# Output projections of the last two token blocks ahead of the rest of an FFN, and an RMS scaling that reads PSUM

## The chip, the cores and the metric
The kernel runs on one core of a Trainium2 chip. Times are device microseconds of one execution, from the first instruction to the last. The kernel before was timed in three runs: median 3093.57 us, 3091.24 to 3095.78.

## The reference, cut to what matters
One decoder layer on 2048 tokens of width 1024, in float32, with a final norm:

```python
h = rms_norm(x, norm1_g)
p = h @ w_in                                   # combined projection of three head groups
mix = concat(mlstm(p), rwkv7(p), diff_attn(p)) # 256 + 256 + 512 columns
x = x + mix @ w_out
h = rms_norm(x, norm2_g)
x = x + square(relu(h @ w_ff_up)) @ w_ff_down  # 1024 -> 4096 -> 1024
return rms_norm(x, final_g)
# rms_norm(x, g) = x * rsqrt(mean(x*x, -1) + eps) * g
```

## The kernel before
Activations stand transposed: features on the 128 partitions, tokens along the free axis. The 2048 tokens are four blocks c = 0..3 of T = 512, and the trunk's state of a block is eight tiles `x` of 128 x 512. A float32 product is made of three products of rounded float32 (`mm3`, lines 182 to 184, and `prod`, lines 1223 to 1225): each operand is split into a high part (ACT, line 174) and a low part (POOL or DVE, line 175), and hi·hi, lo·hi and hi·lo are summed in one PSUM bank. So weights take a path of their own: a load of 128 x 512 (`wraw`, class `Weights`, three raw buffers, six of `whi` and `wlo`), ACT, POOL, TensorE.

The first two thirds make the projection and the three head groups. Attention of blocks 2 and 3 runs at the same time as the FFN of blocks 0 and 1 (class `Tail`): `outproj` (line 1113) makes x + mix @ w_out of one block, 192 products with a residual tile (`traw`, loaded at line 1121) added at line 1126; `hidden` the norm; `ffn` the up products (tile `pd`, line 1162) and down products (tile `py`, added into x at line 1174) of sixteen feature groups fb; `final` (line 1185) the last norm and the stores. `norm` takes squares on ACT (lines 155, 158), adds them on DVE (159), sums over partitions on TensorE with a matrix of ones (162), makes the reciprocal root (164, 134 to 137), spreads it over the partitions by a product with a diagonal matrix (144, 145), copies that out of PSUM (168) and scales (1194 on DVE, 1191 and 1192 on ACT and POOL).

Blocks 2 and 3 come last, and their FFN is made with a Strassen-Winograd scheme of seven products per step (class `Wino`) on the 2 x 2 blocks made of token block and feature half. `first(x2)` norms block 2; `second` norms block 3 (scalings at line 1231) and makes the token operands: differences such as t2 = b11 + (b22 - b12) (lines 1256 to 1272), each split into high and low. `up` runs eight steps with weights in a ring `wr` of 512 KB tiles (loads `wr<-in_wu`; differences of weights at lines 1286 to 1293), `down` four steps with `wr` and a second ring `wr2` (`wr<-in_wd`), token tiles read back from DRAM (`x<-act`), and sums `acc`. The tail of `down` is `final(2)` and `final(3)`.

The order in which each engine runs its instructions is fixed when the program is built: a scheduler takes instructions by priority, and those under `tc.high_priority()` come as soon as their operands and buffers allow by its own reckoning. Each engine then runs its list strictly in order. A buffer is reused when its last reader is through. Memory is given out in pools: a pool opened after another is closed takes its place, and its first writes wait for the readers of what stood there. Before, attention's memory is free at fb = 8 of `ffn(x1)`, by when the pools `wr`, `tx2` and `th2` take it; the two out-projections are generators that are stepped between the feature groups 9 to 15 and share the weight ring and the `traw` ring with the FFN. Loads are issued from the queues of SP and ACT (line 42).

## Time and profile before

| what | us |
|---|---|
| median of three runs | 3093.57 |
| lowest, highest | 3091.24, 3095.78 |
| the profiled execution | 3098.3 |
| its span (first to last record) | 3096.6 |

The engines' busy shares of that span are PE 94%, DVE 63%, ACT 42%, POOL 35%. The profile is of one execution, so its stretches add up to its own time. Times in the rows count from the span's start. FFN(x1) ends at about 2363.4 us, up runs from there to 2714, down to 3062.5. A matrix product of the rows below that lasts 0.39 us is issued every 0.23 us, since they overlap; to count them, divide a full stretch by its number of products. [...]

### The profile page before, as it was taken

To read this page: it belongs to the slowest core of one execution; us is meant where nothing else is said; L and a number is where in the kernel's file an instruction comes from. 1 tells how busy PE (TensorE), PEld (TensorE's weight loads), DVE (VectorE), ACT (ScalarE), POOL (GpSimd) and SP (SyncE) were. 2 spreads that over 40 slices of the span, in tenths; PEclk is the share of its full clock that TensorE was granted. 3 is DMA by queue.
4 is the path that set the end of the run, shared out by engine and by line. 5 is a ranking of instruction groups with operands and counts; after the bars stand their busy time and mean duration, and the time that the engine had idled before them with its cause. 6 is when DMAs were issued, how large, how long until landed. Compare 5 with 4: busy or idle time off the path is not lost. (4 is left out here: it accounts for less than half of the span.)

```text
span 3096.6 us, 47520 instructions
## 1 busy us (share of the span) xinstructions
PE 2898.9 (94%) x16848; PEld 2376.1 (77%) x16848; DVE 1947.5 (63%) x4355; ACT 1297.8 (42%) x2571; POOL 1069.5 (35%) x1023
## 2 busy tenths in 40 slices
PE   8999999999999889999999999987996899979996
PEld 7886887778878667888888788876784688858884
DVE  6587878678772556555555756443435756657787
ACT  5343234323322445444444544443343545434433
POOL 4344444333333114333433333323453322112232
PEclk9999999999999899999999999998998999989998
DMA  8445332643543553533446334424442344474431
GB/s 298 134 136 199 86 98 74 215 120 89 184 127 117 163 140 99 138 101 103 123 113 169 96 106 119 109 69 140 130 140 78 106 150 159 140 258 146 143 116 55
DMA packets 317096, 409.15 MB, mean 132 GB/s; under 512 B 102421, under 2 KB 164150, under 8 KB 315834
## 3 DMA queue, kind: packets, MB, share of 16 engines
q1 hardware_dynamic: 229002, 283.81, 30.0%
q10 hardware_dynamic: 87856, 122.31, 13.0%
q8 instruction: 133, 2.18, 0.3%
q14 instruction: 105, 0.86, 0.1%
HBM read 298.24 MB, written 107.76 MB: 131 GB/s over the span
## 5 line engine op out<-in xcount | busy, mean ns | idle before, releaser
L175 POOL TENSOR_TENSOR wlo<-wraw,whi 128x512 fp32r<-128x512 f32 (+2 forms) x432 | 591.6, 1381 | 825.4 <-ACT whi L174 545.4
L174 ACT ACTIVATE whi<-wraw 128x512 fp32r<-128x512 f32 (+2 forms) x432 | 267.1, 625 | 336.9 <-PE pd L183 98.5
L175 POOL TENSOR_TENSOR wlo<-wr,whi 128x512 fp32r<-128x512 f32 x104 | 148.6, 1430 | 486.6 <-ACT whi L174 401.4
L182 PE MATMUL pd<-hh,whi 128*128 128x512 f32 x768 | 303.2, 399 | 12.2 <-ACT hh L174 12.1
L183 PE MATMUL pd<-hl,whi 128*128 128x512 f32 x768 | 303.9, 396 | 0.0
L1174 DVE TENSOR_TENSOR x<-py,x 128x512 f32<-128x512 f32 x256 | 174.5, 688 | 203.8 <-PE py L184 203.2
L184 PE MATMUL pd<-hh,wlo 128*128 128x512 f32 x768 | 299.9, 395 | 0.0
L1030 DVE TENSOR_SCALAR_CACHE_REDUCE E<-pS 128x512 f32<-128x512 f32 (+4 forms) x320 | 185.8, 607 | 153.3 <-PE pS L1027 87.5
L174 ACT ACTIVATE whi<-wr 128x512 fp32r<-128x512 f32 x224 | 140.1, 630 | 273.6 <-PE pd L1224 135.8
L182 PE MATMUL pd<-hhi,whi 128*128 128x512 f32 x544 | 224.2, 416 | 7.4 <-ACT hhi L279 7.4
L184 PE MATMUL pd<-hhi,wlo 128*128 128x512 f32 x544 | 223.5, 413 | 0.2 <-POOL wlo L175 0.2
L183 PE MATMUL pd<-hlo,whi 128*128 128x512 f32 x544 | 223.2, 412 | 0.4 <-POOL hlo L175 0.3
L182 PE MATMUL py<-ah,whi 128*128 128x512 f32 x512 | 205.7, 402 | 1.5 <-DVE x L1174 1.1
L183 PE MATMUL py<-al,whi 128*128 128x512 f32 x512 | 202.6, 396 | 0.6 <-DVE al L175 0.6
L184 PE MATMUL py<-ah,wlo 128*128 128x512 f32 x512 | 200.8, 396 | 0.0
L1037 ACT ACTIVATE E<-E,nm 128x128 f32<-128x128 f32 (+15 forms) x128 | 153.7, 1201 | 96.0 <-DVE nm L1033 80.1
L182 PE MATMUL pd<-whi,hhi 128*128 128x256 f32 (+1 forms) x640 | 188.3, 295 | 1.3 <-ACT gates L372 1.3
L183 PE MATMUL pd<-wlo,hhi 128*128 128x256 f32 (+1 forms) x640 | 188.4, 294 | 0.0
L184 PE MATMUL pd<-whi,hlo 128*128 128x256 f32 (+1 forms) x640 | 187.0, 292 | 0.0
L1056 PEld LDWEIGHTS pO<-Vt,PT 128*128 128x128 f32 x1088 | 151.9, 202 | 36.1 <-ACT PT L1053 25.8
L182 PEld LDWEIGHTS pd<-hh,whi 128*128 128x128 f32 x768 | 144.9, 190 | 43.9 <-issue 12.5
L1056 PE MATMUL pO<-Vt,PT 128*128 128x128 f32 x1088 | 160.4, 290 | 18.8 <-ACT PT L1053 18.8
(445 smaller groups left out, 7204.5 us busy)
## 6 DMA issues: line engine op xcount, KB each, us to landing
act<-x SPq DMA_DIRECT2D x96, 256.0 KB, 2.1
wraw<-in_wu ACTq DMA_DIRECT2D x64, 256.0 KB, 3.2
wraw<-in_wu SPq DMA_DIRECT2D x64, 256.0 KB, 3.1
wraw<-in_wd ACTq DMA_DIRECT2D x64, 256.0 KB, 3.3
wraw<-in_wd SPq DMA_DIRECT2D x64, 256.0 KB, 3.1
x<-act SPq DMA_DIRECT2D x56, 256.0 KB, 2.8
x<-act ACTq DMA_DIRECT2D x56, 256.0 KB, 2.8
wraw<-in_wi ACTq DMA_DIRECT2D x48, 256.0 KB, 3.5
```

What stands on the lines that cost most here:

```text
L174: nc.scalar.activation(hi, src, AF.Copy)
L175: lo_eng.tensor_tensor(lo, src, hi.bitcast(F32), ALU.subtract)
L182: nc.tensor.matmul(out, sh, mh, start=(i == 0), stop=False)
L183: nc.tensor.matmul(out, sh, ml, start=False, stop=False)
L184: nc.tensor.matmul(out, sl, mh, start=False, stop=(i == n - 1))
L1030: V.tensor_scalar(E[:, k0:k0 + w], s_[:, :w], 0.125, None, ALU.mult, ALU.max, accum_out=mb[:, j:j + 1])
L1037: A.activation(E[:, :n], E[:, :n], AF.Exp, bias=nm, accum_out=l)
L1056: PE.matmul(o[:, 0:P], pt[:, b * P:(b + 1) * P], vt[:, kb], start=(kb == 0), stop=(kb == i))
L1174: nc.vector.tensor_tensor(x2[d], ps, x2[d], ALU.add)
```

## The change
The out-projections of blocks 2 and 3 are no longer stepped through `ffn(x1)`. At fb = 8 both are written one after the other, with a `Weights` object of their own (pool `tw2` in attention's memory, two raw buffers) and a ring `xr` of three for residual and mixed tiles. The norms of x2 and x3 and the operands b11, b21, t2 and t3 (`first`, `second`) follow right behind them, ahead of the rest of `ffn(x1)`. The operands t4, t1 and c22 are made by a new `third` behind `final(1)`. The ring `wr` takes the place of `tw2` and has five buffers rather than six. In `down` the token splits use the pool `th2` rather than one of their own, four groups of token tiles are in use rather than five, and the sixth group of sums stands in a freed slot. The last two norms are written out: `squares` takes the squares of finished sums during the last step, `rstd` sums them on TensorE (also over several tiles in one accumulation) and `scale` multiplies straight from the PSUM tile of the broadcast, block 2 on DVE alone, block 3 with two of its eight tiles on POOL. All stores there are issued by SP.

```diff
--- before.py
+++ after.py
@@ -187,8 +187,8 @@
-    def __init__(s, tc, e, wp, bufs=6, width=512):
-        s.tc, s.e, s.wp, s.bufs, s.width = tc, e, wp, bufs, width
+    def __init__(s, tc, e, wp, bufs=6, width=512, raws=3):
+        s.tc, s.e, s.wp, s.bufs, s.width, s.raws = tc, e, wp, bufs, width, raws
@@ -198,7 +198,7 @@
-                raw = s.wp.tile([P, s.width], F32, name="wraw", tag="wraw", bufs=3)
+                raw = s.wp.tile([P, s.width], F32, name="wraw", tag="wraw", bufs=s.raws)
@@ -1082,7 +1082,7 @@
-        s.hp = p(s.hctx, "th", bufs=10)
+        s.hp = p(s.hctx, "th", bufs=8)
@@ -1098,26 +1098,27 @@
-    def load(s, c, pool=None):
+    def load(s, c, pool=None, raw=None):
...
         for k in range(KT):
-            r = s.raw()
+            r = (raw or s.raw)()
...
-    def outproj(s, c, m, x2, g, pd=None, keep=None):
+    def outproj(s, c, m, x2, g, w=None, raw=None, pd=None, keep=None):
...
+        get = (w or s.w).get
         for u in range(4):
-            w = s.w.get(s.wo[u], 256)
+            w = get(s.wo[u], 256)
             for j in range(2):
                 d = 2 * u + j
-                xr = s.raw()
+                xr = (raw or s.raw)()
...
-    def second(s, x2, x3, hp, tp):
+    def second(s, x2, x3, hp):
 
...
         with s.tc.high_priority():
             s.rms(x3)
-            b11, b21, b12, b22 = x2[:4], x2[4:], x3[:4], x3[4:]
-            t2, t3, t1, t4 = [], [], [], []
+            b11, b12, b22 = x2[:4], x3[:4], x3[4:]
+            s.t2, s.t3 = t2, t3 = [], []
             for k in range(4):
                 V.tensor_tensor(b12[k], b22[k], b12[k], ALU.subtract)
                 V.tensor_tensor(b11[k], b12[k], b11[k], ALU.add)
                 t2 += s.cut(b11[k:k + 1], [tl.hl(hp)], (V,))
             for k in range(4):
-                t3 += s.cut(b12[k:k + 1], [tl.hl(hp)], (G, V))
+                t3 += s.cut(b12[k:k + 1], [tl.hl(hp)], (V,))
+
+    def third(s, x2, x3, tp):
...
+        with s.tc.high_priority():
+            b11, b21, b12, b22 = x2[:4], x2[4:], x3[:4], x3[4:]
+            t1, t4 = [], []
             for k in range(4):
                 V.tensor_tensor(b21[k], b21[k], b11[k], ALU.subtract)
                 t4 += s.cut(b21[k:k + 1], [tl.hl(tp)], (V,))
             for k in range(4):
                 V.tensor_tensor(b12[k], b22[k], b11[k], ALU.subtract)
                 t1 += s.cut(b12[k:k + 1], [(tl.slot(2, F32R), tl.slot(3, F32R))], (V,))
-            c22 = s.cut(b22, [tl.hl(), tl.hl()] + [(tl.slot(1, F32R), tl.slot(1, F32R)) for _ in range(2)], (G, V))
-        s.ops = [s.b11, t2, s.b21, t3, t1, t4, c22]
+            c22 = s.cut(b22, [tl.hl(tp), tl.hl(tp)] + [(tl.slot(1, F32R), tl.slot(1, F32R)) for _ in range(2)], (G, V))
+        s.ops = [s.b11, s.t2, s.b21, s.t3, t1, t4, c22]
...
 
@@ -1309,7 +1318,7 @@
             with tc.high_priority():
-                w = s.blocks(s.wr, 6, [tl.wu[fb + 8 * m][:, 4 * k:4 * k + 4] for m in range(2) for k in range(2)])
+                w = s.blocks(s.wr, 5, [tl.wu[fb + 8 * m][:, 4 * k:4 * k + 4] for m in range(2) for k in range(2)])
...
-    def down(s, ap, ar, wr2):
+    def down(s, ap, hp, wr2):
...
-        grp = [2, 3, 0, 4, 5]
...
-        acc = [[ap.tile([P, T], F32, name="acc", tag=f"a{p}{q}") if p < 6 else tl.slot(1) for q in range(4)] for p in range(7)]
+        grp = [2, 3, 0, 4]
...
+        acc = [[ap.tile([P, T], F32, name="acc", tag=f"a{p}{q}") if p < 5 else tl.slot(5 if p == 5 else 1) for q in range(4)] for p in range(7)]
         with tc.high_priority():
             for p, c, d in ((2, 0, 0), (5, 0, 4), (6, 1, 0)):
                 for q in range(4):
@@ -1383,8 +1392,8 @@
             with tc.high_priority():
-                f = [s.factors(s.blocks(r, b, [tl.wd[2 * st + i + 8 * k][:, :, T * m:T * m + T] for m in range(2) for k in range(2)]))
-                     for i, (r, b) in enumerate(((s.wr, 6), (wr2, 5)))]
+                f = [s.factors(s.blocks(r, 5, [tl.wd[2 * st + i + 8 * k][:, :, T * m:T * m + T] for m in range(2) for k in range(2)]))
+                     for i, r in enumerate((s.wr, wr2))]
@@ -1396,7 +1405,7 @@
                 for k in range(4):
...
                         w = s.unit(ws[k // 2][:, k % 2 * T:k % 2 * T + T], V if k % 2 else G)
-                        b = (ar.tile([P, T], F32R, name="uh", tag="uh"), ar.tile([P, T], F32R, name="ul", tag="ul"))
+                        b = tl.hl(hp)
@@ -1414,9 +1423,61 @@
-                if last and p == 5:
-                    tl.final(2, acc[2] + acc[5], (1, 5))
-        tl.final(3, acc[6] + x22, (2, 4, 7))
+                    if last and p == 2:
+                        n2 = s.squares(tl.np.tile([P, T], F32, name="nacc", tag="nacc", bufs=1), acc[2], True)
+                    if last and p == 4:
+                        n3 = s.squares(ap.tile([P, T], F32, name="nacc"), x22, True)
+                    if last and p == 5:
+                        s.squares(n2, acc[5], False)
+                        r2 = s.rstd([n2], 1)
+        with tc.high_priority():
+            sq = [n3]
+            for q in range(4):
+                sq.append(tl.slot(2))
+                A.activation(sq[-1], acc[6][q], AF.Square)
+            s.scale(3, x22 + acc[6], s.rstd(sq, 0), tl.slot(3), (1, 3))
+        s.scale(2, acc[2] + acc[5], r2, None, ())
+
+    def squares(s, n, x, new):
...
+        nc = s.tc.nc
+        for i, t in enumerate(x):
+            y = n if new and i == 0 else s.tl.raw()
+            nc.scalar.activation(y, t, AF.Square)
+            if y is not n:
+                nc.vector.tensor_tensor(n, n, y, ALU.add)
+        return n
+
+    def rstd(s, sq, i):
...
+        nc, e, tl = s.tc.nc, s.e, s.tl
+        ps = s.bank(i)
+        for j, t in enumerate(sq):
+            for tt in range(4):
+                nc.tensor.matmul(ps[:, tt:tt + 1], t[:, tt * P:(tt + 1) * P], e.ones[:, 0:1], start=j + tt == 0, stop=j == len(sq) - 1,
+                                 skip_group_check=True)
+        sm = tl.np.tile([P, 3, 4], F32, name="nsm", tag="nsm", bufs=2)
+        nc.vector.tensor_scalar(sm[:, 0], ps[:, 0:4], 1.0 / D, NORM_EPS, ALU.mult, ALU.add)
+        rsqrt(nc, e, sm[:, 1], sm[:, 0], sm[:, 2])
+        ps = s.bank(i)
+        bcast_rows(nc, e, tl.raw(), ps, sm[:, 1])
+        return ps
+
+    def scale(s, c, x, r, t, pool):
...
+        nc, e, tl = s.tc.nc, s.e, s.tl
+        g = lambda k: e.vf[:, V_FG + k:V_FG + k + 1]
+        order = [(k + 4) % KT if c == 3 else k for k in range(KT)]
+        for i in pool:
+            nc.scalar.activation(x[i], x[i], AF.Copy, scale=g(order[i]))
+        if pool:
+            nc.scalar.copy(t, r)
+        for i, k in enumerate(order):
+            if i in pool:
+                nc.gpsimd.tensor_tensor(x[i], x[i], t, ALU.mult)
+            else:
+                nc.vector.scalar_tensor_tensor(x[i], x[i], g(k), r, ALU.mult, ALU.mult)
+            nc.sync.dma_start(tl.out[c, :, k], x[i])
 
@@ -1540,33 +1601,29 @@
             actx.close()
             with tc.using_default_side("right"):
                 pq = [ctx.enter_context(tc.tile_pool(name=f"pq{i}", bufs=2, space=PSUM)) for i in range(2)]
-                wr = ctx.enter_context(tc.tile_pool(name="wr", bufs=1))
                 tl.xp2 = ctx.enter_context(tc.tile_pool(name="tx2", bufs=1))
-                hp2 = rctx.enter_context(tc.tile_pool(name="th2", bufs=8))
-            op = tl.outproj(2, tl.load(2, hp2), x2, (0, 1), pq[0], e.x2d[0])
-        if 8 < fb < 12:
-            next(op)
-        if fb == 12:
-            list(op)
-            wn = Wino(tl, wr, pq)
+                hp2 = ctx.enter_context(tc.tile_pool(name="th2", bufs=8))
+                w2 = Weights(tc, e, rctx.enter_context(tc.tile_pool(name="tw2", bufs=1)), raws=2)
+            raw2 = lambda: w2.wp.tile([P, T], F32, name="xr", tag="xr", bufs=3)
+            for _ in tl.outproj(2, tl.load(2, hp2, raw2), x2, (0, 1), w2, raw2, pq[0], e.x2d[0]):
+                pass
+            wn = Wino(tl, pq)
             wn.first(x2)
-            op = tl.outproj(3, tl.load(3, hp2), x3, (4, 5), pq[1], e.x2d[1])
-        if 12 < fb < 15:
-            next(op)
-        if fb == 15:
-            list(op)
+            for _ in tl.outproj(3, tl.load(3, hp2, raw2), x3, (4, 5), w2, raw2, pq[1], e.x2d[1]):
+                pass
+            wn.second(x2, x3, hp2)
     tl.final(1, x1, (2, 5))
     tl.actx.close()
-    tp = tl.hctx.enter_context(tc.tile_pool(name="tp", bufs=4))
-    wn.second(x2, x3, hp2, tp)
+    rctx.close()
+    with tc.using_default_side("right"):
+        wn.wr = ctx.enter_context(tc.tile_pool(name="wr", bufs=1))
+    tp = tl.hctx.enter_context(tc.tile_pool(name="tp", bufs=6))
+    wn.third(x2, x3, tp)
     wn.up()
     tl.hctx.close()
-    rctx.close()
     wr2 = ctx.enter_context(tc.tile_pool(name="wr2", bufs=1))
     ap = ctx.enter_context(tc.tile_pool(name="acc", bufs=1))
-    with tc.using_default_side("right"):
-        ar = ctx.enter_context(tc.tile_pool(name="au", bufs=5))
-    wn.down(ap, ar, wr2)
+    wn.down(ap, hp2, wr2)
 
```

How the change moves the instructions is seen at three places. The first is TensorE in attention's last head. `pO`, `pT` and `pS` are attention's tiles, `py` and `pd` the FFN's down and up products. The lines with a minus stand there before, and no more after.

```order
-L182 MATMUL pd<-hh,whi 128x512
-L183 MATMUL pd<-hl,whi 128x512
-L184 MATMUL pd<-hh,wlo 128x512
 L1056 MATMUL pO<-Vt,PT 128x128 x4
 L1026 MATMUL pS<-Kst,Qd 128x512
```

In all, 48 products of one feature group's up part leave the last head of attention and stand behind it; up to there the two lists are the same.

The second place is DVE around the norm of x3 (`nacc` its squares, `nsm` the reciprocal root, `traw` the diagonal matrix). Before, it stands behind the last norm of x1 (L1194), and the operands of up follow:

```order
L1194 SCALAR_TENSOR_TENSOR x<-x,vf,nacc 128x512 x6
L159 TENSOR_TENSOR nacc<-nacc,traw 128x512 x7
L164 TENSOR_SCALAR nsm<-nps 128x4
L135 TENSOR_TENSOR nsm<-nsm 128x4
L136 SCALAR_TENSOR_TENSOR nsm<-nsm 128x4
L137 SCALAR_TENSOR_TENSOR nsm<-nsm 128x4
L144 TENSOR_TENSOR traw<-ident,nsm 128x512
L1231 SCALAR_TENSOR_TENSOR x<-x,vf,nacc 128x512 x8
L1256 TENSOR_TENSOR x<-x 128x512 x2
```

After, it stands behind out-projection 3 (L1127 is its add), with subtractions of up's weights (`wr`) between its steps:

```order
L1127 TENSOR_TENSOR x<-pd,xr 128x512
L159 TENSOR_TENSOR nacc<-nacc,traw 128x512
L164 TENSOR_SCALAR nsm<-nps 128x4
L1295 TENSOR_TENSOR wr<-wr 128x4x128 x2
L135 TENSOR_TENSOR nsm<-nsm 128x4
L136 SCALAR_TENSOR_TENSOR nsm<-nsm 128x4
L1296 TENSOR_TENSOR wr<-wr 128x4x128 x2
L137 SCALAR_TENSOR_TENSOR nsm<-nsm 128x4
L144 TENSOR_TENSOR traw<-ident,nsm 128x512
L1232 SCALAR_TENSOR_TENSOR x<-x,vf,nacc 128x512 x8
L1257 TENSOR_TENSOR x<-x 128x512 x4
```

The norm of x3 has moved ahead of 714 products of FFN(x1), and on TensorE its two products (L162, L145) now stand directly behind out-projection 3. Behind the last product of FFN(x1) stand, after, 85 products of up ahead of the first that takes t1.

The third place is DVE at the end of the program. Before, `acc` are the tiles of block 2 and `x` those of block 3:

```order
L144 TENSOR_TENSOR traw<-ident,nsm 128x512
L1194 SCALAR_TENSOR_TENSOR acc<-acc,vf,nacc 128x512 x6
L159 TENSOR_TENSOR nacc<-nacc,traw 128x512 x7
L164 TENSOR_SCALAR nsm<-nps 128x4
L135 TENSOR_TENSOR nsm<-nsm 128x4
L136 SCALAR_TENSOR_TENSOR nsm<-nsm 128x4
L137 SCALAR_TENSOR_TENSOR nsm<-nsm 128x4
L144 TENSOR_TENSOR traw<-ident,nsm 128x512
L1194 SCALAR_TENSOR_TENSOR x<-x,vf,nacc 128x512 x5
```

After, `py` and `pd` are the two broadcasts in PSUM, and the first four `x` scaled are block 2's second half:

```order
L1420 TENSOR_TENSOR x<-pd,x 128x512 x2
L1479 SCALAR_TENSOR_TENSOR acc<-acc,vf,py 128x512 x4
L1479 SCALAR_TENSOR_TENSOR x<-x,vf,py 128x512 x4
L1460 TENSOR_SCALAR nsm<-pd 128x4
L135 TENSOR_TENSOR nsm<-nsm 128x4
L136 SCALAR_TENSOR_TENSOR nsm<-nsm 128x4
L137 SCALAR_TENSOR_TENSOR nsm<-nsm 128x4
L144 TENSOR_TENSOR traw<-ident,nsm 128x512
L1479 SCALAR_TENSOR_TENSOR x<-x,vf,pd 128x512 x6
```

The seven adds of squares have gone from between the two scalings, and block 2's eight scalings stand ahead of block 3's root.

## Rows read from the trace of the kernel before

**Rows 1.** The chain that ended last, share of the span by engine, from the page

```profile
PE 28%; DVE 2%; DMA 1%; issue 0%; POOL 0%; ACT 0%; DVEq 0%; ACTq 0%; SPq 0%; POOLq 0%
```

**Rows 2.** Busy time by stretch; columns as in the first line

```profile
core 0: us, PE busy (x) PEld busy (x) DVE busy (x) ACT busy (x) POOL busy (x), PEclk, DMA share, GB/s
2022.30:2045.60 23.30, 23.30 (x120) 19.54 (x120) 13.43 (x38) 8.81 (x14) 8.62 (x7) 1.00 0.40 112
2064.20:2076.70 12.50, 9.65 (x68) 8.02 (x68) 8.52 (x23) 6.96 (x11) 0.00 (x0) 0.98 0.00 1
2098.50:2110.30 11.80, 0.00 (x0) 0.03 (x1) 2.65 (x5) 1.31 (x3) 0.00 (x0) 0.50 0.72 245
2110.30:2125.00 14.70, 14.70 (x56) 11.61 (x57) 8.19 (x12) 9.50 (x17) 2.92 (x3) 0.88 0.46 143
2125.00:2200.00 75.00, 75.00 (x329) 61.51 (x328) 21.12 (x29) 24.80 (x42) 36.74 (x29) 1.00 0.43 133
...
2250.00:2363.40 113.40, 111.94 (x482) 89.82 (x480) 46.59 (x60) 46.42 (x79) 57.16 (x43) 1.00 0.41 127
2363.40:2425.00 61.60, 24.85 (x78) 16.64 (x79) 47.85 (x67) 23.49 (x42) 20.53 (x12) 0.64 0.09 34
2425.00:2714.00 289.00, 289.00 (x1262) 236.83 (x1262) 184.31 (x258) 142.02 (x239) 60.81 (x45) 1.00 0.44 152
2714.00:2750.00 36.00, 14.61 (x52) 11.13 (x51) 9.99 (x16) 8.91 (x16) 0.50 (x1) 0.75 0.97 351
...
3062.50:3096.60 34.10, 5.08 (x13) 2.58 (x12) 20.42 (x28) 7.42 (x13) 8.53 (x6) 0.55 0.33 123
```

**Rows 3.** Timeline, end of attention: start, duration, engine, line, operation, [idle before, releaser]

```profile
2098.58 0.82 ACTq L42 DMA_DIRECT2D wr<-in_wu  x2
...
2107.47 1.29 DVE L1287 TENSOR_TENSOR wr<-wr 128x512 f32<-128x512 f32 x2 [1.12 <-DMA wr<-in_wu]
...
2109.58 0.63 ACT L174 ACTIVATE hh<-traw 128x512 fp32r<-128x512 f32 x1 [9.55 <-DMA mixT<-ot]
```

**Rows 4.** Timeline, from the last add of FFN(x1) to the start of up

```profile
2363.81 0.68 DVE L1174 TENSOR_TENSOR x<-py,x 128x512 f32<-128x512 f32 x1
...
2374.27 6.17 DVE L1194 SCALAR_TENSOR_TENSOR x<-x,vf,nacc 128x512 f32<-128x512 f32 x6 [3.30 <-ACT nacc L168]
...
2380.54 0.63 ACT L155 ACTIVATE nacc<-x 128x512 f32<-128x512 f32 x1 [6.30 <-DMA out<-x]
...
2404.76 0.79 PE L1223 MATMUL pd<-hh,whi 128*128 128x512 f32 x1 [11.39 <-ACT hh L174]
```

**Rows 5.** Timeline, start of down

```profile
2720.05 0.79 PE L1223 MATMUL pd<-uh,whi 128*128 128x512 f32 x1 [5.54 <-ACT uh L174]
...
2735.60 0.56 ACTq L42 DMA_DIRECT2D wr<-in_wd  x1
...
2749.42 0.80 PE L1223 MATMUL pd<-uh,whi 128*128 128x512 f32 x1 [15.85 <-ACT whi L174]
```

**Rows 6.** Timeline, from the last product to the end

```profile
3062.18 0.39 PE L1225 MATMUL pd<-uh,wlo 128*128 128x512 f32 x1
...
3066.51 6.17 DVE L1194 SCALAR_TENSOR_TENSOR acc<-acc,vf,nacc 128x512 f32<-128x512 f32 x6 [2.42 <-ACT nacc L168]
...
3072.77 0.63 ACT L155 ACTIVATE nacc<-x 128x512 f32<-128x512 f32 x1 [6.30 <-DVE acc L1194]
...
3086.19 6.51 DVE L1194 SCALAR_TENSOR_TENSOR x<-x,vf,nacc 128x512 f32<-128x512 f32 x5 [2.85 <-ACT nacc L168]
```

**Rows 7.** Durations by line: ns min/median/max, first and last start

```profile
L1194 DVE SCALAR_TENSOR_TENSOR acc<-acc,vf,nacc x6: 737/739/1854, 3066.5 to 3071.9; 128x512 f32<-128x512 f32 x6
...
L1174 DVE TENSOR_TENSOR x<-py,x x256: 672/691/694, 1213.4 to 2363.8; 128x512 f32<-128x512 f32 x128
```

**Rows 8.** Loads: queue, count, KB each, median us to landing

```profile
wraw<-in_wo ACTq DMA_DIRECT2D x32, 256.0 KB, 2.9
...
wr<-in_wu ACTq DMA_DIRECT2D x16, 512.0 KB, 5.8
```

**Rows 9.** POOL's split of weights, the page's group: busy, mean ns

```profile
L175 POOL TENSOR_TENSOR wlo<-wraw,whi 128x512 fp32r<-128x512 f32 (+2 forms) x432 | 591.6, 1381 | 825.4 <-ACT whi L174 545.4
```

6 lines of the change are left out of this document (4 added, 2 removed).

## The prediction
> **What bounds the kernel now.** I read the chain of waits first: it is TensorE nearly from end to end (28% PE, 2% DVE, 1% DMA by its lines) [rows 1], so the time is the number of products by their pace, plus the stretches in which PE stands still. The table by stretches shows these. In a full stretch PE is busy all the time at full clock, 329 products in 75.00 us or 1262 in 289.00: 0.228 us each [rows 2]. Four stretches in the last third are not full: 11.8 us behind the end of attention with no product at all, 61.6 us at the start of the Strassen-Winograd up part (PE 24.85), 36 us at the start of its down part (14.61), and 34.1 us behind the last product (5.08) [rows 2]. The timelines of these four say what each waits for, and the change edits all four.
>
> **Stretch 1, the end of attention to the end of FFN(x1) (2098.5 to 2363.4 = 264.9 us).** Before, attention's last store and five half-megabyte loads of `wr` start together; PE begins its out-projection 11.8 us later [rows 2, 3]. The change adds no products but moves 48 of FFN(x1) (L1162) from attention's last head to behind it: 48 x 0.228 = 11 us more here. They were not free there: up to 2045.6 PE is full (23.3 of 23.3 us for a query block), so without them attention should end sooner. Its own chain sets a floor: the last blocks with almost no FFN take 12.5 us with PE at 9.65 [rows 2]. I take 9.5 of the 11 us back, bounds 0 and 11.
> Both out-projections (192 products each) now run without FFN products between them, on weights with two raw pieces in flight. Working: the first two output blocks end 1.5 + 18.5 us after attention (48 x 0.228 = 11, the rest the store, load and split of `mixT`, 6 us with no `wr` loads ahead, where before ACT stood 9.55 us between the copy of the last output and the first split at 2109.58 [rows 3]), the other six take 144 x 0.232 = 33.4. Out-projection 3 has its tokens early: 12.4 + 33.4, with some 4 us for the norm of x2 and switches. Then comes a **new wait**. On DVE the norm of x3 (L164 to L144) has four weight subtractions of the up part (L1295, L1296) between its steps, and these wait for `wr` loads that, by their place in memory, can be issued only when the last product of out-projection 3 is through. PE has the norm's L145 queued ahead of all FFN products. Before, the second pair of such operations (L1287, on five loads issued from 2098.58 on) began 8.9 us after that issue [rows 3]; with 1.3 us for it, 0.9 for L137 and L144, one or two of issue and add, and the slow clock after it, I take 14 us, bounds 10 and 20. The clock's share: after the wait at 2110.3, the next 56 products took 14.7 us at a mean clock of 0.88, against 12.8 at full pace [rows 2]. The remaining 714 FFN products take 163.9. Sum: 20 + 33.4 + 45.8 + 4 + 14 + 163.9 = 281, so **+16 here, -9.5 for attention: +7** (bounds 0 and +18).
>
> **Stretch 2, start of up.** Before, after the last FFN product the norm of x1 with its scaling and stores, then the norm of x3, which begins only when x1's stores let its buffers go (2380.54), then its scalings and all differences and splits follow one another, and the first product that needs them waits until 2404.76 [rows 4]. In 61.6 us there are 78 products: 78 x 0.228 = 17.8, so 43.8 are lost here, and with the ones started before, 47.8. The change puts norm, scaling and the operands b11, t2 and t3 behind out-projection 3, under FFN(x1), where DVE is busy 46.59 of 113.4 us [rows 2]; 8 scalings, 8 differences and 8 splits of about 0.7 us each, 17 us, are hidden there. Behind the last FFN product 85 up products stand ready (85 x 0.228 = 19 us) ahead of the first that needs t1. From the last add to t1 there remain the norm of x1 (2363.81 to 2374.27, 10.5 us), its scaling of 6.2 [rows 4], and some 14 differences and splits at 0.7, about 27 us in all. So 8 are lost in place of 47.8: **-40** (bounds -34 and -45).
>
> **Stretch 3, start of down.** Before, PE waits 5.54 us for token blocks and then 15.85 for the first piece of the second weight ring, whose loads start only at 2735.60, behind the token loads, with the DMA engines 97% busy [rows 2, 5]. Afterwards, by the order, that ring's first two loads wait only for the second-last stage of the last up step, 61 products (14 us) ahead of use, and 24 rather than 12 products cover the first token wait. The row of 15.85 goes to about 2, the one of 5.54 to 2.8: **-16.5** (bounds -8, if the same bytes at 351 GB/s push the gap later, and -20, the sum of both and the slow clock).
>
> **Stretch 4, the end.** Before, behind the last product at 3062.57 stand: scaling of block 2 from 3066.51 to 3072.68, then from the first square at 3072.77 on the squares, sums, rsqrt and broadcast of block 3, its scaling from 3086.19 (6.51), and stores to the end of the span, 3096.6 [rows 6]: 34.0 us. Afterwards the squares of block 3's first half are summed under the last products, those of the other half go to PE as 16 columns, and no copy stands ahead of DVE's scaling. But DVE's order now has block 2's eight scalings ahead of block 3's rsqrt. Working from the last product: four adds to +1.3, eight scalings at 0.8 to +7.7, rsqrt to +10.6, broadcast to +12.7, six scalings to +18.5 (with POOL's two beside it up to 19.5), last store 3.9: +22.5. **-11** (bounds -8, both scalings at the disturbed price, and -13).
> The price of 0.8: out of SBUF the scaling took 739 ns undisturbed and 1854 with POOL at work beside it; an add out of PSUM took 691 [rows 7]. I take it near the latter, a little more for three operands. [...]
>
> **What the edits cost elsewhere.** Five `wr` buffers instead of six, four token groups instead of five, eight `th` slots instead of ten: nothing as long as DMA (44% busy in up) and DVE (184 of 289) cover it [rows 2]. If a load comes late once in each of eight up steps and four down steps, by 1 to 2 us, it costs up to 20. I take **+4** (bounds 0 and +20).
>
> **Sum.** +7 - 40 - 16.5 - 11 + 4 = -56.5 against the profiled 3098.3: 3041.8. The profiled execution is 4.7 above the median of 3093.57, so the forecast is **3037**.
>
> **Rivals.** (a) *The out-projections wait for their weights.* With two raw pieces, a pair of pieces takes its landing plus 2.0 us (ACT's 0.63 and POOL's 1.38 [rows 3, 9]), and feeds 24 products, 5.57 us: it decides at a landing of 3.6 us. The median was 2.9, with DMA 43% busy in the same stage [rows 2, 8], which speaks for my forecast; the profile has landings of 5.8 for the bigger `wr` loads. At 4.5 us each of 16 pairs loses 0.9: +15, 3052. [...]
> (b) *The same, far worse, and slower than before.* The whole gain of 56.5 is gone at 3.5 us lost for each of 16 pairs, so from a landing of 7.1 us. That needs the DMA engines as full as in the stretch at 97%, where half-megabyte loads and token loads were queued; at 8 us it is 16 x 4.4 = +71, 3108. Against it: the out-projections ask for 1.5 MB in 11 us, about the 133 GB/s that the stage moved before [rows 2].
> (c) *The new wait behind out-projection 3 is long and attention ends no sooner.* 20 us instead of 14, and 0 instead of 9.5: +15.5, 3052. For it: the floor of the chain may already set the last head; against it the full PE until 2045.6.
> (d) *The starts of up and down close only by half.* Before, the first square of x3's norm waited 6.30 us for x1's stores [rows 4]; if t1 waits for x1's buffers in the same way, and the down gap only moves: +15 and +8, 3060.
> (e) *The end gains nothing*, because block 2's scalings and POOL's share stay ahead of block 3: +11, 3048.
>
> **How the numbers follow.** Forecast 0.58 (3018 to 3048 with its own bounds), (a) 0.10, (b) 0.05, (c) 0.10, (d) 0.10, (e) 0.04; 0.03 for a gain above all bounds. The range 3016 to 3064 holds the forecast, (a), (c), (e) and half or more of (d). A measurement of this kernel tells about 0.2% (6 us) from none; only (b) and a sum of several rivals come near: faster 0.92, same 0.03, slower 0.05.
>
> **What would show it.** In the profile after: the last transposes of attention 9 us sooner; PE full through both out-projections except one wait of 12 to 16 us behind the second, ended by DVE's L144 and, through it, by a `wr` load; PE near full from the last FFN product on, with one gap of less than 10 us; no gap above 5 us at the start of down; 22 to 23 us from the last product to the end. Gaps that come again each 5.6 us in the out-projections, or each 36 us in up, would be the smaller rings and make the forecast wrong.

## The result and the profile after

The changed kernel took 3057.44 us in the median of four runs (3051.4 to 3062.33), the kernel before 3094.68 (3091.24 to 3096.8): a ratio of 0.988, with an interval of 0.9859 to 0.990, or 37 us less. The forecast was 3037 with a range of 3016 to 3064: right in sign and within the range, but the gain is two thirds of the 56.5 us that were summed up. The profiled execution took 3062.33 us, its span is 3060.6, 36.0 below the 3096.6 of before.

Busy time of the changed kernel by stretch, with the columns of [rows 2]. The limits are the stations of the table further below; PEclk is the share of its full speed that TensorE's clock was granted.

```profile
core 0: us, PE busy (x) PEld busy (x) DVE busy (x) ACT busy (x) POOL busy (x), PEclk, DMA share, GB/s
2088.70:2097.50 8.80, 0.46 (x3) 0.19 (x2) 0.61 (x1) 1.74 (x3) 0.00 (x0) 0.50 0.55 173
2097.50:2209.50 112.00, 100.27 (x394) 77.84 (x394) 44.73 (x58) 37.15 (x62) 42.89 (x33) 0.92 0.56 174
2209.50:2223.00 13.50, 3.12 (x11) 2.03 (x12) 5.01 (x11) 0.63 (x1) 1.01 (x1) 0.65 0.51 175
2223.00:2360.50 137.50, 137.50 (x606) 113.72 (x605) 60.07 (x77) 55.93 (x95) 70.75 (x52) 1.00 0.31 92
2360.50:2384.50 24.00, 14.63 (x41) 10.40 (x40) 19.44 (x26) 9.72 (x18) 11.31 (x7) 0.79 0.11 33
...
2405.00:2712.00 307.00, 299.66 (x1293) 244.56 (x1292) 194.28 (x277) 153.53 (x257) 71.51 (x52) 0.98 0.43 148
2712.00:2740.00 28.00, 27.85 (x121) 22.26 (x120) 19.19 (x25) 12.95 (x23) 5.54 (x4) 1.00 1.01 355
...
3040.40:3060.60 20.20, 6.36 (x36) 4.23 (x34) 11.34 (x21) 1.93 (x4) 3.50 (x3) 0.65 0.55 208
```

The big holes of [rows 2] are gone: up has PE at 299.66 of 307.00 us from its start on, the start of down is full although DMA is as busy as before (355 GB/s against 351), and the end is 20.2 us in place of 34. Three new stretches stand in their place, all ahead of up: both out-projections together are busy 100.27 of 112.00 at a mean clock of 0.92, 13.5 us behind them are almost empty, and near the end of FFN(x1) 41 products take 24 us.

By stations (last transposes of attention, first product of out-projection 2, last add of out-projection 3, end of the broadcast L145 behind it, last add of FFN(x1), last add of up, last add of down, end of the span), with what the prediction's steps come to between the same points:

| stretch, us | before | after | change | predicted change |
|---|---|---|---|---|
| start to attention's last copy | 2099.4 | 2089.2 | -10.2 | -9.5 |
| copy to last add of FFN(x1) | 264.4 | 315.6 | +51.2 | +16 |
| to last add of up | 344.5 | 307.2 | -37.3 | -40 |
| to last add of down | 354.3 | 328.4 | -25.9 | -16.5 |
| to the end | 34.0 | 20.2 | -13.8 | -11 |
| smaller rings | | | none seen | +4 |

So attention's end, the start of down and the end gave what was forecast or more, and the start of up 2.7 us less. The miss of 20 us comes from the second line, where 35 us more than forecast were lost. That line is, after: out-projections to the last product 120.2 from the copy (102.3 forecast), the wait behind them 13.5 (14), the rest of FFN(x1) 181.8 (163.9). Two steps were wrong by 17.9 each.

The first of them in the timeline of the changed kernel, one turn of each of the two raw weight buffers in out-projection 2 (start, duration, engine, line, operation, idle and releaser). The rows of ACT's queue and SP's queue are the loads:

```profile
2129.13 0.33 ACTq L42 DMA_DIRECT2D wraw<-in_wo  x1
...
2131.17 0.50 SPq L42 DMA_DIRECT2D wraw<-in_wo  x1
2132.55 0.63 ACT L174 ACTIVATE whi<-wraw 128x512 fp32r<-128x512 f32 x1 [1.64 <-DMA wraw<-in_wo]
...
2133.32 1.29 POOL L175 TENSOR_TENSOR wlo<-wraw,whi 128x512 fp32r<-128x512 f32 x1 [2.33 <-ACT whi L174]
...
2134.64 0.33 ACTq L42 DMA_DIRECT2D wraw<-in_wo  x1
...
2135.90 0.63 ACT L174 ACTIVATE whi<-wraw 128x512 fp32r<-128x512 f32 x1 [2.72 <-DMA wraw<-in_wo]
...
2136.66 1.29 POOL L175 TENSOR_TENSOR wlo<-wraw,whi 128x512 fp32r<-128x512 f32 x1 [2.06 <-ACT whi L174]
...
2137.98 0.33 SPq L42 DMA_DIRECT2D wraw<-in_wo  x1
```

Each of these loads is issued in the moment in which POOL is through with the piece that stood in the buffer: 5.5 us a turn on ACT's side (2129.13 to 2134.64), 6.8 on SP's (2131.17 to 2137.98). Over both out-projections 22 of the 30 loads behind the first two come so, within 0.2 us; the eight others come 0.8 to 3.6 us later, seven of them on ACT's queue. Two pieces feed 24 products, 5.5 us, and the turns last from 5.1 to 9.3 us. ACT stands waiting for a load before 26 of the 32 splits of a weight. PE's own waits are not one in each turn: behind the first product there are ten of 0.3 to 3.0 us, 11.5 in all, and the products between them come at a mean clock of 0.92.

The second, the timeline at the end of FFN(x1) in the changed kernel:

```profile
2363.34 2.71 ACT L174 ACTIVATE hh<-x 128x512 fp32r<-128x512 f32 x5 [4.65 <-DVE x L1258]
...
2370.26 0.47 PE L182 MATMUL py<-ah,whi 128*128 128x512 f32 x1 [4.64 <-ACT traw L1164]
...
2372.81 3.43 DVE L1271 TENSOR_TENSOR x<-x 128x512 f32<-128x512 f32 x2
...
2378.11 0.79 PE L182 MATMUL py<-ah,whi 128*128 128x512 f32 x1 [3.28 <-DVE x L1175]
```

`hh<-x` are splits of up's operands, five in a row on ACT, L1258 and L1271 the sums and differences that make them on DVE. Two of these took 3.43 us, with POOL's splits beside them. FFN's own last activation (L1164) and the adds that let its PSUM go (L1175) stand behind them in the queues, and PE waits 4.64 and 3.28 us for these. Behind both waits the products come every 0.43 us rather than 0.23 for a while: the granted clock is 0.63 from 2370.2 to 2374.8 and 0.52 from 2378.1 to 2384.5.

The wait behind out-projection 3 is the one that was forecast (load issue, the root's chain on DVE, the broadcast on PE):

```profile
2210.24 0.82 ACTq L42 DMA_DIRECT2D wr<-in_wu  x2
...
2213.67 0.16 DVE L164 TENSOR_SCALAR nsm<-nps 128x4 f32<-128x4 f32 x1 [1.21 <-PE nps L162]
...
2217.28 1.29 DVE L1295 TENSOR_TENSOR wr<-wr 128x512 f32<-128x512 f32 x2 [3.45 <-DMA wr<-in_wu]
...
2220.16 0.69 DVE L144 TENSOR_TENSOR traw<-ident,nsm 128x512 f32<-128x512 f32 x1
2220.90 2.07 PE L145 MATMUL nps<-traw,ones 128*128 128x512 f32 x2 [7.27 <-DVE traw L144]
```

And the end, which answers to [rows 6]: the sums of squares on PE, block 2's eight scalings while block 3's root is made, then block 3's six.

```profile
3041.06 3.63 PE L1457 MATMUL pd<-ones,x 128*128 128x1 f32 x32
3041.26 2.72 DVE L1479 SCALAR_TENSOR_TENSOR acc<-acc,vf,py 128x512 f32<-128x512 f32 x4 [0.17 <-PE py L145]
...
3043.90 2.72 DVE L1479 SCALAR_TENSOR_TENSOR x<-x,vf,py 128x512 f32<-128x512 f32 x4
...
3049.14 2.08 PE L145 MATMUL pd<-traw,ones 128*128 128x512 f32 x2 [4.46 <-DVE traw L144]
...
3051.87 4.04 DVE L1479 SCALAR_TENSOR_TENSOR x<-x,vf,pd 128x512 f32<-128x512 f32 x6 [2.79 <-ACT x L1474]
```

### The profile page after: what moved, and what is told of

It is laid out like the page before. It is cut to its first block, busy times and chain, and to the rows that moved or that the text cites. A ratio compares the mean times of both kernels' runs of the same rounds, so it can differ in the third digit from the quotient of the medians.

```text
span 3060.6 us, 47580 instructions
## 1 busy us (share of the span) xinstructions
PE 2907.0 (95%) x16880; PEld 2383.8 (78%) x16880; DVE 1936.0 (63%) x4358; ACT 1295.7 (42%) x2567; POOL 1063.1 (35%) x1016
## 4 chain that ended last, share of the span: by engine, by line
PE 56%; DVE 5%; DMA 4%; ACT 1%; issue 1%; POOL 1%; SPq 0%; ACTq 0%; DVEq 0%; POOLq 0%
PE pd L183 5%; PE pd L182 5%; PE pd L184 5%; PE pd L1224 5%; PE pd L1225 5%; PE pd L1226 5%; PE pO L1056 4%; PE py L182 4%; PE py L183 4%; PE py L184 3%; PE pS L1026 2%; PE pS L1027 2%; PE pT L1051 2%; PE py L1226 2%; PE py L1224 2%; PE py L1225 2%
## 5 line engine op out<-in xcount | busy, mean ns | idle before, releaser
L182 PE MATMUL pd<-hh,whi 128*128 128x512 f32 x768 | 304.0, 402 | 18.6 <-ACT whi L174 9.7
L183 PE MATMUL pd<-hl,whi 128*128 128x512 f32 x768 | 305.2, 398 | 1.0 <-DVE hl L175 1.0
L184 PE MATMUL pd<-hh,wlo 128*128 128x512 f32 x768 | 300.4, 397 | 1.4 <-POOL wlo L175 1.4
L1175 DVE TENSOR_TENSOR x<-py,x 128x512 f32<-128x512 f32 x256 | 174.9, 688 | 196.0 <-PE py L184 195.4
L1224 PE MATMUL pd<-hh,whi 128*128 128x512 f32 x560 | 221.0, 396 | 1.5 <-DVE x L1348 1.3
L1226 PE MATMUL pd<-hh,wlo 128*128 128x512 f32 x560 | 221.5, 396 | 0.0
L1225 PE MATMUL pd<-hl,whi 128*128 128x512 f32 x560 | 221.5, 396 | 0.0
L182 PEld LDWEIGHTS pd<-hh,whi 128*128 128x128 f32 x768 | 146.5, 192 | 52.6 <-issue 11.2
```

Source lines behind the costliest of these rows:

```text
L182: nc.tensor.matmul(out, sh, mh, start=(i == 0), stop=False)
L183: nc.tensor.matmul(out, sh, ml, start=False, stop=False)
L184: nc.tensor.matmul(out, sl, mh, start=False, stop=(i == n - 1))
L1175: nc.vector.tensor_tensor(x2[d], ps, x2[d], ALU.add)
L1224: mm(ps, sh, mv[0], start=start, stop=False, skip_group_check=True)
L1225: mm(ps, sh, mv[1], start=False, stop=False, skip_group_check=True)
```

## The experiments

All kernels here are the changed kernel with an edit. Their medians can't be set against one another to a few us: in ten kernels with the same order up to there, the stretch from the first to the last transposes of attention took from 1039.0 to 1051.2 us, longest in the changed kernel itself. The stretches behind it agree to 2 or 3 us where nothing was edited, so the verdicts rest on them, each from one profiled execution. All in us; the columns are out-projections (first product to last add), the wait behind them, FFN(x1) to its last add, up, down, and the end.

| kernel | median | out-proj. | wait | FFN | up | down | end |
|---|---|---|---|---|---|---|---|
| changed kernel | 3057.4 | 112.0 | 13.5 | 181.8 | 307.2 | 328.4 | 20.2 |
| e1, three raws, two xr | 3053.0 | 115.0 | 13.6 | 181.9 | 306.9 | 328.3 | 20.2 |
| e1b, three raws, five pairs | 3046.5 | 99.1 | 13.7 | 182.0 | 306.9 | 328.5 | 20.2 |
| e3, first weights plain | 3047.1 | 109.2 | 8.0 | 183.1 | 308.8 | 325.9 | 20.2 |
| e4, scaling out of SBUF | 3046.9 (one run) | 111.0 | 13.6 | 181.9 | 308.3 | 327.0 | 21.6 |
| e5, operand slots swapped | 3053.6 | 112.1 | 13.5 | 174.8 | 307.9 | 332.0 | 20.2 |
| e6, e1b + e3 + e5 | 3037.3 | 102.0 | 10.1 | 175.5 | 307.9 | 333.2 | 20.2 |
| e6x, and four xr | 3040.8 | 99.1 | 9.3 | 175.7 | 305.7 | 334.8 | 20.2 |
| e7, old end | 3076.8 (one run) | 113.4 | 13.6 | 182.0 | 306.9 | 327.7 | 33.8 |
| e8, e6x with other swap | 3030.4 | 97.7 | 8.8 | 177.0 | 307.7 | 326.1 | 20.2 |
| e10, one group later | 3052.6 | 107.1 | 14.3 | 158.1 | 306.6 | 328.5 | 20.2 |
| e11, e8 one group later | 3036.0 | 99.0 | 11.8 | 153.6 | 306.5 | 327.8 | 20.2 |
| e12, e8 two groups later | 3027.5 | 97.2 | 8.0 | 134.4 | 306.9 | 327.8 | 20.2 |

### Do the out-projections wait for their weights?

The third raw buffer takes 2 KB per partition, for which another ring gives way: once that of residual tiles, once that of split pieces.

```diff
-                w2 = Weights(tc, e, rctx.enter_context(tc.tile_pool(name="tw2", bufs=1)), raws=2)
-            raw2 = lambda: w2.wp.tile([P, T], F32, name="xr", tag="xr", bufs=3)
+                w2 = Weights(tc, e, rctx.enter_context(tc.tile_pool(name="tw2", bufs=1)), raws=3)
+            raw2 = lambda: w2.wp.tile([P, T], F32, name="xr", tag="xr", bufs=2)
```

That is e1. In e1b the ring xr keeps its three, and the pairs go from six to five:

```diff
-                w2 = Weights(tc, e, rctx.enter_context(tc.tile_pool(name="tw2", bufs=1)), raws=2)
+                w2 = Weights(tc, e, rctx.enter_context(tc.tile_pool(name="tw2", bufs=1)), bufs=5, raws=3)
```

> The changed kernel with three raw weight buffers for the two out-projections in place of two, and, to find the memory, two tiles in the ring for residual and mixed tiles in place of three. Theory A (the out-projections wait for their weights because only two loads can be under way): each of the 16 pairs of pieces gets back what it lost, the two out-projections take 46 us each in place of 54.3 and 54.6 (the wait between them, 3.0 us, may stay), so 12 to 18 us less, about 3042. Rival B (the weight loads come late because SP's queue has the stores of x2 and x3 and the residual loads ahead of them, or because ACT and POOL split too slowly): the out-projections stay within 3 us of 54 each, and the time within 4 us of 3057.

> As the run before, but the memory is found in the ring of split weights (five pairs of high and low pieces in place of six) and the ring for residual and mixed tiles keeps its three. Theory A: the same gain, 12 to 18 us, and a start of out-projection 2 that is no later than in the changed kernel (8.3 us behind the copy of attention's last output). If the ring of split pieces limits, the gain is some us smaller than with six pairs. Rival B: no gain.

e1 alone would have spoken against theory A (two raw buffers are too few): 115.0 us, no gain. Its gaps are of another kind: the products wait up to 4.96 us for the splits of mixed tiles, which come through the ring that had been cut to two. e1b, with that ring whole, is 12.9 us shorter, at the low end of what theory A expected, and PE is nearly full there:

```profile
2097.40:2196.40 99.00, 94.52 (x394) 73.26 (x394) 45.57 (x57) 36.07 (x62) 44.05 (x33) 0.98 0.63 197
```

The same products and bytes, but 197 GB/s rather than 174 [first table]: DMA was not full (a share of 0.56 in the changed kernel, 0.63 here), the two buffers did not let enough of it be under way. Rival B (SP's queue, or the speed of the splits) falls for these 12.9 us: neither was edited, and in the changed kernel one load on SP's queue in fifteen was issued late. The other runs agree: with two raw buffers the out-projections took 109.2 to 113.4 us, with three, and three or more xr tiles, 97.7 to 102.0 (in the kernels that write them at fb = 8). Six pairs of split pieces with three raw buffers and three xr tiles were not run, so what five pairs cost is not known.

### What is the wait behind out-projection 3?

```diff
-            with tc.high_priority():
+            with tc.high_priority() if fb else ExitStack():
...
-                    with tc.high_priority():
+                    with tc.high_priority() if fb else ExitStack():
```

The first of the two stands around `blocks`, the second around `unit` of up's first step.

> The changed kernel, with the loads and differences of the first up step's weights at ordinary priority, so that the four subtractions L1295 and L1296 stand on DVE behind the norm of x3 (behind L144) and no longer between its steps. Theory: the wait between the last product of out-projection 3 and the next FFN product falls from 13.5 us to about 6 (adds and squares 3.2, sum 1, root 2, diagonal 0.7, broadcast), so 7 us less, about 3050. Rival: DVE waits for the weights a little later, ahead of the scalings, and FFN's splits behind them are late by the same 7 us: no gain.

The wait is 8.0 us in place of 13.5, 5.5 less (7 expected). The timeline of e3: the diagonal matrix is made at once, and the subtractions on up's weights follow, waiting for the loads. FFN(x1) and up are 1.3 and 1.6 us longer, down 2.5 shorter, which the scatter of these stretches covers; the rival's loss of the same 7 us does not show.

```profile
2201.78 0.69 DVE L144 TENSOR_TENSOR traw<-ident,nsm 128x512 f32<-128x512 f32 x1
2202.53 2.08 PE L145 MATMUL nps<-traw,ones 128*128 128x512 f32 x2 [2.66 <-DVE traw L144]
...
2204.30 1.30 DVE L1295 TENSOR_TENSOR wr<-wr 128x512 f32<-128x512 f32 x2 [1.83 <-DMA wr<-in_wu]
```

### Why do up's operands delay the end of FFN(x1)?

In the changed kernel `first` splits b11 and b21 into the pool `th`, whose eight slots hold the tokens of FFN(x1) until the up products of its last group, the last of them at 2360.46; the first of these splits comes at 2347.1. The sum that makes t2 overwrites b11 and so waits for that split, and t3 and the difference of t4 follow. e5 exchanges the memory: b11 and b21 go to `th2`, free behind out-projection 3, and t2 and t3 to `th`.

```diff
-            s.b11 = s.cut(x2[:4], [s.tl.hl() for _ in range(4)], (nc.vector, nc.gpsimd))
-            s.b21 = s.cut(x2[4:], [s.tl.hl() for _ in range(4)], (nc.vector, nc.gpsimd))
...
+            s.b11 = s.cut(x2[:4], [tl.hl(hp) for _ in range(4)], (V, G))
+            s.b21 = s.cut(x2[4:], [tl.hl(hp) for _ in range(4)], (V, G))
...
-                t2 += s.cut(b11[k:k + 1], [tl.hl(hp)], (V,))
+                t2 += s.cut(b11[k:k + 1], [tl.hl()], (V,))
...
-                t3 += s.cut(b12[k:k + 1], [tl.hl(hp)], (V,))
+                t3 += s.cut(b12[k:k + 1], [tl.hl()], (V,))
```

`hp` is the pool `th2`. The two splits go from `first` to `second`, behind the norm of x3.

> The changed kernel, with the memory of two groups of up's operands exchanged: the splits of b11 and b21 go to the pool th2 (free behind out-projection 3), those of t2 and t3 to the pool th (held by the token tiles of FFN(x1) until its last up product). Theory C (in the changed kernel b11's split waits for th, and t2, t3 and the differences on top of it wait for b11, so all of it falls between the last up and the last down products of FFN(x1), where it delays them): 8 splits and 8 sums and differences move forward, the gaps of PE between 2361 and 2380 (9.4 us and some 4 at the low clock) fall to less than half, 6 to 10 us less, about 3049. Rival D (these operations come late for another reason, their place in the scheduler's list or DVE's own load): gaps and time stay within 3 us.

FFN(x1) is 7.0 us shorter, and of the waits of 4.64 and 3.28 us at its end nothing is left:

```profile
2365.00:2400.00 35.00, 33.88 (x146) 26.64 (x144) 26.99 (x37) 15.90 (x28) 13.29 (x10) 1.00 0.16 46
```

Rival D (the place in the list, or DVE's own load, makes them late) falls for these waits: the edit puts the two splits later in the program, and with the memory that was free the work still came earlier. The sums for t2 (L1258) start from 2236.0 to 2238.4, in the changed kernel from 2348.5 to 2362.6. But it now crowds another place. PE has a new wait of 2.52 us near the start of FFN(x1), for the low part of a weight:

```profile
2242.65 1.22 PE L184 MATMUL py<-ah,wlo 128*128 128x512 f32 x2 [2.52 <-POOL wlo L175]
```

That subtraction on POOL began at 2235.74 and lasted 6.86 us, against 1.27 for the next one, while DVE ran ten operations without a pause, nine of them sums and differences of up's operands. So the 7.0 us are what is left of a larger gain. The median is only 4 us lower, and down is 3.6 longer, 332.0, as then in e6 and e6x too. Theory F is that the first loads of down's second ring go to memory that `th` held, and that t3 is read last one product later in up's last step than b21, which had stood there.

### The end

e4 lets DVE's last six scalings read the copy of the broadcast in SBUF, which POOL uses anyway:

```diff
-                nc.vector.scalar_tensor_tensor(x[i], x[i], g(k), r, ALU.mult, ALU.mult)
+                nc.vector.scalar_tensor_tensor(x[i], x[i], g(k), t if pool else r, ALU.mult, ALU.mult)
```

> The changed kernel, with DVE's six last scalings of block 3 reading the broadcast from the copy in SBUF that POOL uses already, rather than from PSUM; all else is the same. Theory E (two operands in SBUF make DVE wait while POOL multiplies beside it, an operand in PSUM spares it that): the first three of the six take about 1.85 us in place of 0.74, as three of six did in the kernel before; the scalings take 7 us in place of 4.5 and the stretch behind the last product 22.5 to 23.5 in place of 20.2. [...]

The end is 1.4 us longer, 21.6. The six scalings, in the changed kernel and then in e4 (ns min, median, max):

```profile
L1479 DVE SCALAR_TENSOR_TENSOR x<-x,vf,pd x6: 740/740/746, 3051.9 to 3055.2; 128x512 f32<-128x512 f32 x6
```

```profile
L1479 DVE SCALAR_TENSOR_TENSOR x<-x,vf x6: 739/740/1851, 3035.1 to 3040.5; 128x512 f32<-128x512 f32 x6
...
L1477 POOL TENSOR_TENSOR x<-x x2: 1261/1484/1708, 3035.1 to 3036.3; 128x512 f32<-128x512 f32 x2
```

With the broadcast in PSUM none is disturbed, though the first four ran beside POOL's two multiplications; with it in SBUF the first two of the six, which did so, took 1851 and 1743 ns, as in [rows 7], and POOL's second took 1708 in place of 1268. Undisturbed, PSUM and SBUF cost the same, 740 ns. Theory E (an operand in PSUM spares DVE POOL's company) holds, though two of the six were hit and not three.

e7 puts the old end back (`final(2)` and `final(3)`), all else as changed.

```diff
-                    if last and p == 5:
-                        s.squares(n2, acc[5], False)
-                        r2 = s.rstd([n2], 1)
...
-            s.scale(3, x22 + acc[6], s.rstd(sq, 0), tl.slot(3), (1, 3))
-        s.scale(2, acc[2] + acc[5], r2, None, ())
+                if last and p == 5:
+                    tl.final(2, acc[2] + acc[5], (1, 5))
+        tl.final(3, acc[6] + x22, (2, 4, 7))
```

> The changed kernel with the old end of the program (the last norms of blocks 2 and 3 as before: sums of squares on DVE behind the last product, copy of the broadcast to SBUF, ACT's queue issuing half of the stores). Theory: the stretch behind the last product goes back from 20.2 to 34 us and nothing else moves, so 14 us more. Rival (the squares that the change takes during the last step cost part of what the end gains, since DVE is full there): the down part gets 2 to 6 us shorter with the old end, and the loss is only 8 to 12.

One run took 3076.81 us. The last add of up starts at 2713.6 there, the last add of down at 3041.3, and its span is 3075.1: 327.7 for down, against 328.4, and 33.8 for the end. So the early squares cost down nothing that could be told from its scatter (0.7 us), and the gain of 13.6 is the end's own. Its three scalings of `acc` show POOL's company again:

```profile
L1195 DVE SCALAR_TENSOR_TENSOR acc<-acc,vf,nacc x3: 739/1745/1853, 3045.0 to 3048.4; 128x512 f32<-128x512 f32 x3
```

### Do the gains add up, and is there a better kernel?

> Three raw weight buffers with five split pairs, the first up weights at ordinary priority, and the operand slots exchanged, all in one. If the three causes are separate, their gains add up: 12.9 in the out-projections, 5.5 behind them, 7.0 at the end of FFN(x1), 25 in all, about 3032. If they overlap (the first up weights then come late, or the freed operands crowd DVE where the norm of x3 stands), 15 to 20.

> As the run before, with four tiles rather than three in the ring for residual and mixed tiles. Two in place of three had cost 16 us against the same number of raw buffers (115.0 against 99.1 for both out-projections). Theory: what is left there over 384 products at 0.228 (99.1 against 87.6) is waiting for mixed tiles at the start of each, and the fourth tile takes 3 to 6 us of it. Rival: DMA is the limit by then, and nothing changes.

e6 is 20 us below the changed kernel, not 25: the out-projections give 10.0, the wait 3.4, FFN(x1) 6.3, and down takes 4.8 back, as in e5. A fourth xr tile brings the out-projections to 99.1 from 102.0, which is no more than e1b had with three; that theory is not borne out, and by its median e6x is no better than e6.

e8 has the edits of e6x, and chooses the operands by when they are last read: b11 and t3 in `th2`, b21 and t2 in `th`. Against e5's form:

```diff
-            s.b21 = s.cut(x2[4:], [tl.hl(hp) for _ in range(4)], (V, G))
+            s.b21 = s.cut(x2[4:], [tl.hl() for _ in range(4)], (V, G))
...
-                t3 += s.cut(b12[k:k + 1], [tl.hl()], (V,))
+                t3 += s.cut(b12[k:k + 1], [tl.hl(hp)], (V,))
```

> As e6x (three raw buffers, five split pairs, four xr tiles, first up weights at ordinary priority), but with another exchange of the operands' memory: b11 and t3 are split into th2, b21 and t2 into th. In e5, e6 and e6x the down part took 332 to 335 us in place of 328.4. Theory F (the first loads of the second weight ring go to memory that the operands in th hold until the last up step reads them for the last time; with t3 there that is the fourth of seven products, with b21 the third, as in the changed kernel): the down part goes back to 328 to 329 us, the end of FFN(x1) stays at 175 to 178, and the time is some 5 us below e6x, 3032 to 3036. Rival (the longer down part has another cause, such as DMA that is busy at its start in any case): it stays at 332 or more.

Down is back at 326.1, and the median is 3030.43, 0.9784 of the kernel before with an interval of 0.9758 to 0.981. Theory F, that down's loss hangs on which operand is last read out of `th`, is shown as far as one exchange can show it, and the traces agree: the one wait of PE in down, 3.14 us in e5, 4.58 in e6 and 4.67 in e6x, for the high part of a weight, is gone in e8. The second ring's first load is issued 8.7 to 10.9 us behind the last add of up in these three, 6.2 in the changed kernel and 4.0 in e8. FFN(x1) stays short (177.0), but the operand work is not out of the way:

```profile
2216.51 1.22 PE L184 MATMUL py<-ah,wlo 128*128 128x512 f32 x2 [5.17 <-POOL wlo L175]
```

PE waits 5.17 us for one subtraction on POOL that lasted 6.84 us, beside ten operations of DVE in a row that read two tiles each. No run took this work off DVE or POOL, so what these 5 us are worth is open. This kernel beats both: 65.6 us below the kernel before that ran beside it, 27 below the changed kernel's median.

The last question is the 48 products that left attention's last head. e10 writes the out-projections one feature group later, e11 and e12 do so to e8 with one and two groups.

```diff
-        if fb == 8:
+        if fb == 9:
```

> The changed kernel with both out-projections written one feature group later (fb = 9), so that the products of one more group stand in attention's last head and not behind it. Theory G (in the last head PE is full only up to some 45 us before its end; the 48 products that the change took out there were nearly at full price, and a group put back fills idle time only in part): attention ends 8 to 16 us later, the stretch of FFN behind the out-projections is 22 us shorter (96 products), net 0 to 10 us less, 3047 to 3057. Rival (the chain of attention's last head sets its end, and products between cost nothing): attention ends where it did, and the time falls by the whole 22 us.

> e8 with the out-projections one feature group later, as in e10. There the end of attention went 10.1 us back and FFN behind the out-projections got 23.7 us shorter, 5 us less by the medians. If that gain is independent of the four edits of e8: 5 to 10 us below e8, 3020 to 3026. Rival (the up group taken from behind the out-projections had covered their operands' splits, which now crowd it): no gain, 3028 to 3033.

> e8 with the out-projections two feature groups later. In e10 PE was nearly full until attention's end but for some 8 us, so a second group should cost attention as much as it spares behind it: within 3 us of e11. Rival (there is still idle time to fill): 5 us or more below e11.

First and last transposes of attention in the changed kernel, then in e12:

```profile
L1068 PE MATMUL pT<-ident,osb x64: 270/272/476, 1037.5 to 2088.7; 128*128 128x128 f32 x64
```

```profile
L1068 PE MATMUL pT<-ident,osb x64: 270/272/474, 1040.6 to 2125.1; 128*128 128x128 f32 x64
```

From e8 to e11 FFN behind the out-projections gets 23.4 us shorter and attention ends 25.0 later; from e8 to e12 it is 42.6 and 42.6. What is taken out on one side is paid on the other, as far as a stretch that varies by 12 us can show it. PE is busy 66.6 of attention's last 80 us in e8, 69.0 in e11 and 70.2 in e12: the products of two groups fill under 4 us of idle time there. e10 alone looked cheaper, 10.1 us later for 23.7 spared, but against a changed kernel whose attention was the longest of ten, and its gain of 5 us did not come again in e11 (3036.0, with 3025.4 to 3037.5). e12's 3027.5 can't be told from e8's 3030.4. The rival, that products in the last head cost nothing, falls.

## Why the prediction was right in sign and too large in size

**What bounds the kernel.** The shares of [rows 1] add up to 31% of the span, so that chain was followed back through the last third only, and "nearly from end to end" is more than it shows. The four stretches lie in this third, and the sum doesn't use the rest.

**Attention's end, -9.5.** Measured -10.2. The reasoning (PE full, so a product taken out is a product saved) is borne out by e11 and e12. That the number agrees so well is partly luck: this stretch varies by 12 us, and the executions compared are one of each kernel.

**The out-projections, 102.3 from the copy; measured 120.2.** The step that failed is that the out-projections run at full pace on two raw buffers. Its ground stands in rival (b), and (a)'s small chance rested on it too: "the out-projections ask for 1.5 MB in 11 us, about the 133 GB/s that the stage moved before". It counted weights and residuals and left out the token loads and the stores of x2 and x3, each as large as the residuals. A block moves 4 + 2 + 2 + 2 MB, 10.5 million bytes in the 44 us of 192 products at 0.228, an estimate of 240 GB/s at full pace and not 133; before, the same bytes were spread over the FFN products between. So the landing was not that of [rows 8]:

```profile
wraw<-in_wo ACTq DMA_DIRECT2D x32, 256.0 KB, 3.5
wraw<-in_wo SPq DMA_DIRECT2D x32, 256.0 KB, 3.6
```

These medians, over all four blocks, stand at the point from which rival (a) decides (3.6 us), against 2.9 from which the forecast was made (SP's queue, which [rows 8] leaves out, had 3.2), and single landings of the two last blocks are longer, as the 4.7 us from 2131.17 to 2135.90. Rival (a) held the mechanism and the price of +15. The runs bear out the cure that it implies: 12.9 us came back with a third buffer (e1b); on PE the gaps were ten and not regular, and it is ACT that stood waiting at nearly every piece. Rival (a) had a chance of 0.10 and should have been part of the forecast. The other 5.0 us stay open; in e1b PE still waits 4.3 us, most of it for mixed tiles and their splits.

**The wait behind out-projection 3, 14.** Measured 13.5, at the place and by the chain that were named, and e3 shows that 5.5 of it are the weight subtractions.

**The rest of FFN(x1), 163.9; measured 181.8.** The step that failed: "8 scalings, 8 differences and 8 splits of about 0.7 us each, 17 us, are hidden there". DVE did have the time, but the operations did not have their memory. The change shows `th` cut from ten buffers to eight, and the prediction priced that ring at "nothing" without asking which operands wait for it (whether ten would have done was not run). The trace accounts for 17 of the 17.9: PE stands idle 9.7 us, in the two long waits and three of less than 1 us; the products behind the two long ones, at the low clock, cost 4.6 more; and 2.7 are twelve up products that ran ahead of FFN's last ones (12 x 0.228; they are missing from the next stretch). e5 takes both long waits away and gives only 7.0 us back; part of the rest went into its new wait near the start.

**Start of up, -40; measured -37.3**, including those 2.7, so 34.6 without them. The products without need of t1 covered most of the norm of x1; the waits left there are 2.85, 3.15 and 1.34 us, 7.3 in all against 8 lost by forecast, and behind the second one the products come at the low clock again (0.50 from 2412 to 2420). That the gain comes from x3's norm and the operands moved ahead is read from the two traces: no run undoes that alone.

**Start of down, -16.5; measured -25.9.** The bound of -20, "the sum of both and the slow clock", was added up wrong: the two waits alone are 21.4 us, and [rows 2] has 52 products in 36 us, which is 24.1 lost. All of it came back. The second ring's loads start earlier as forecast, 6.2 us behind the last add of up in place of 27.3; DMA is still full (1.01), but PE has no wait there.

**The end, -11; measured -13.8**, and -13.6 by e7. The scalings last 0.74 us and follow one another every 0.66, not 0.8, and POOL does not disturb them: the fourteen take 9.5 us in place of 11.2. Besides, the prediction's working has a slip of 1 us: from +12.7, six scalings at 0.8 end at +17.5 and not +18.5. An operand in PSUM made the scalings no dearer: medians of 740 and 743 ns with it, 740 without (e4).

**Smaller rings, +4.** Nothing: with five `wr` buffers up is within 2 us of 307 in every kernel, and behind its first 30 us PE has no wait above 0.3 us.

The misses: +17.9, -0.5, +17.9, +2.7, -9.4, -2.8, -0.7 and -4 make +21, and -56.5 + 21 is the 36 us that were measured. Two errors of 18 us were half hidden by terms that had been too cautious, 17.4 us in all (down 9.4, the rings 4, the end 2.8, attention 0.7, the wait 0.5). Without these the time would have been some 3075 us and outside the range: that it fell within it is luck of this kind.
